# A transformer layer in fp32r matmuls: moving operands stored with even columns ahead of odd ones, and read alternately

## The chip, the cores and the metric

The kernel runs on one core of a Trainium2 chip. The metric is the device time of one execution in microseconds; smaller is better. Before the change it is 909.54 us, the median of 3 runs (909.48 to 910.15).

## The reference

One layer of a hybrid block, 512 tokens, width 1024, fp32 throughout. What is computed, cut to its core:

```python
h = rms_norm(x, mix_norm_pre)
xa, ga, q, k, v, f_logit, g_a, g_b = split(h @ w_in)
hr = rg_lru(causal_dwconv(xa, conv_a_w, conv_a_b), ...)       # recurrence over tokens, width 1280
y_a = gelu(ga) * hr
y_b = forgetting_attention(q, k, v, f_logit + b_forget)       # 16 heads of 64, causal
merged = sigmoid(g_a + b_merge[0]) * (y_a @ w_proj_a) + sigmoid(g_b + b_merge[1]) * (y_b @ w_proj_b)
x = x + rms_norm(merged @ w_out, mix_norm_post)
h = rms_norm(x, ffn_norm_pre)
gate, val = split(causal_dwconv(h @ w_up, conv_f_w, conv_f_b))  # 2 x 3072
x = x + rms_norm((gelu(gate) * val) @ w_down, ffn_norm_post)
```

## The kernel before

**Matmuls.** Each fp32 operand `a` is split into a high part (`ah`, rounded to fp32r by a cast on ACT) and a low part (`al = a - ah`, a subtraction on DVE), and a product is made of three matmuls, high by high, high by low and low by high (`mm3`, L218 to L220; the Strassen products L429 to L432; `out_matmuls` L1175 to L1177; `down_step` L1459 to L1461). A matmul has a stationary operand of 128 by 128, which a weight load (PEld) brings into the array, and a moving operand of 512 or 256 columns that streams past it from SBUF. It writes to a bank of PSUM.

**Stages.** The program goes through them in this order; PE's work follows one after another.

- xa: the input projection of the recurrent branch, weights stationary, tokens moving (512 columns, `project`); with it the gates of the recurrence (`gate_mm`).
- v: tokens stationary, weights moving. ga and pa: weights stationary, tokens moving.
- The merge gates ma and mb by Strassen's scheme (`Halved`, `Pair.product`): blocks of 256 tokens moving.
- Attention over pairs of heads: q, k, scores (`scores`, L1006), softmax on DVE and ACT, transposes of the probabilities (`pt`, L1042), A times V (`av`, L1066 and L1067), then pb.
- wo: merged tokens stationary (`mh`, `ml`), columns of `w_out` moving.
- up: the first six column tiles in halves of 256 tokens (`project_half`, L230 to L233), the others by Strassen's scheme, 84 matmuls of 256 columns a pair of tiles.
- down: seven products of Strassen's scheme, each in six steps of 12 matmuls; tokens stationary (`ah`, `al`), columns of `w_down` moving, 512 wide (the last in halves of 256).

**What sets the order.** The code's order, with a scheduler that places instructions as buffers come free, and three hand-ordered stretches (`manual_schedule`): the head, the merge gates and the Strassen part of up into down. SP issues nearly all loads; POOL issues the sums for the Strassen weights of down between DRAM buffers (`background`) and 42 adding transfers (L365). `fetch` loads and splits weights one or two units ahead of their use. `offset` tiles shift pools to chosen places in SBUF.

**Who makes the operands.** `hh`, `hl`: casts and subtractions from transposed blocks (`turned_hi`, `turned_lo`); `xh`, `xl` L519 and L520; `yh`, `yl` L773 and L774; `yb` L1073 and L1074; q and k in `halves` L992 and L993; `mh`, `ml` L1160 and L1161; the down projection's `ah` L1427 and `al` (`sub`, L325); weights in `Split` L172 and L175.

Of the kernel before, what the change touches and what calls it, by code (L numbers as in the profile page):

```python
# [57 lines left out]
NU = 3  # L58
HALO = rg_halo()
# [4 lines left out]
def kernel(  # L64
# [27 lines left out]
    cpool.tile([P, 120], F32, name="offset0")  # L92
# [17 lines left out]
    pool.memset(epst, EPS)  # L110
    cpt = cpool.tile([P, NC], F32, name="cpt")
# [110 lines left out]
    def project(dst, unit, ah, al, lo=0, hi=S):  # L222
        wh, wl = unit
        for k in range(KD):
            mm3(dst[:, lo:hi], wh[:, k], wl[:, k], ah[:, k, lo:hi], al[:, k, lo:hi], k == 0, k == KD - 1)

    def project_half(dst, unit, ah, al, c):
        wh, wl = unit
        for k in range(KD):
            pe.matmul(dst[:, c], wh[:, k], ah[:, k, c], start=k == 0, stop=False)  # L230
            pe.matmul(dst[:, c], wh[:, k], al[:, k, c], start=False, stop=False)
        for k in range(KD):
            pe.matmul(dst[:, c], wl[:, k], ah[:, k, c], start=False, stop=k == KD - 1)  # L233

    def rstd_of(ss, name):
        sd = small.tile([P, 1], F32, tag="sd", name=f"sd_{name}")
        act.activation(out=sd, in_=ss, func=AF.Sqrt, bias=epst, scale=1.0 / D)
# [65 lines left out]
    def v_mm(u, pv, w):  # L303
        wh, wl = w
        for t in range(NT):
            tok = slice(t * P, (t + 1) * P)
            for i in range(2):
                k = 2 * u + i
                pe.matmul(pv[t], hh[:, k, tok], wh[:, i], start=k == 0, stop=False)
                pe.matmul(pv[t], hh[:, k, tok], wl[:, i], start=False, stop=False)  # L310
                pe.matmul(pv[t], hl[:, k, tok], wh[:, i], start=False, stop=k == KD - 1)
# [29 lines left out]
    class Pair:  # L341
# [77 lines left out]
        def product(self, n, dst, first=False):  # L419
# [8 lines left out]
            for k in range(KH):  # L428
                pe.matmul(dst, wh[:, k], ah[:, k], start=first and k == 0, stop=False, skip_group_check=True)  # L429
                pe.matmul(dst, wh[:, k], al[:, k], start=False, stop=False, skip_group_check=True)  # L430
            for k in range(KH):
                pe.matmul(dst, wl[:, k], ah[:, k], start=False, stop=k == KH - 1, skip_group_check=True)  # L432
# [66 lines left out]
    with ExitStack() as rg:  # L499
        rt, ixt, tt = {}, {}, {}  # L500
        last_act = [None]
        with ExitStack() as r0:
# [47 lines left out]
            def gate_mm(t):  # L550
# [3 lines left out]
                for g, pg in enumerate(pgs):  # L554
                    mm3(pg, gh[:, g], gl[:, g], xh[t], xl[t], True, False)
                    if tl is None:
                        pe.matmul(pg, gh[: 3 * n, 2 + g], th[: 3 * n], start=False, stop=True)
                    else:
                        mm3(pg, gh[:n, 2 + g], gl[:n, 2 + g], th[:n], tl[:n], False, True)
# [11 lines left out]
            with tc.tile_pool(name="pre", bufs=2, side="right", reuse_waits="tile") as pre, ExitStack() as wp:  # L571
# [66 lines left out]
                def by_kind(i, c, kinds):  # L638
                    wh, wl = us[i].parts()
                    for n, (w, h, k0, k1) in enumerate(kinds):  # L640
                        for k in range(k0, k1):
                            pe.matmul(pss[i][:, c], (wh, wl)[w][:, k], (hh, hl)[h][:, k, c],
# [124 lines left out]
        def gate_out(t):  # L767
# [5 lines left out]
            act.copy(yh[t], gl)  # L773
            dve.tensor_tensor(out=yl[t], in0=gl, in1=yh[t].bitcast(F32), op=ALU.subtract)  # L774
# [29 lines left out]
        def forget():  # L804
# [10 lines left out]
            for k in range(KD):  # L815
                pe.matmul(pf[0:48], fw[:, k], hh[:, k], start=k == 0, stop=False)
                pe.matmul(pf[0:48], fw[:, k], hl[:, k], start=False, stop=k == KD - 1)
# [11 lines left out]
            dve.tensor_scalar(out=cum, in0=cum, scalar1=-8.0, scalar2=None, op0=ALU.mult)  # L829
            for b in range(NT):  # L830
                nc.sync.dma_start(cnd[:, PO[b] : PO[b + 1]], cum[:, : PO[b + 1] - PO[b]])
# [42 lines left out]
        for step, (e, half) in enumerate(PA_ORDER):  # L874
# [3 lines left out]
            for i in range(5):  # L878
                k = 5 * half + i
                mm3(pps[e], wh[:, i], wl[:, i], yh[k], yl[k], k == 0, k == TR - 1)  # L880
# [32 lines left out]
    def prep_alloc(p):  # L913
# [71 lines left out]
    with ExitStack() as at:  # L985
# [3 lines left out]
        def halves(ps, name):  # L989
            hi = apool.tile([P, S], F32R, tag=f"{name[0]}h", name=f"h_{name}", bufs=1)  # L990
            lo = apool.tile([P, S], F32R, tag=f"{name[0]}l", name=f"l_{name}", bufs=1)
            rounded.append(act.copy(hi, ps))  # L992
            dve.tensor_tensor(out=lo, in0=ps, in1=hi.bitcast(F32), op=ALU.subtract)  # L993
# [63 lines left out]
        def av(p, pts):  # L1057
# [15 lines left out]
            act.copy(yb[p][:, 0], y)  # L1073
            dve.tensor_tensor(out=yb[p][:, 1], in0=y, in1=yb[p][:, 0].bitcast(F32), op=ALU.subtract)  # L1074
# [3 lines left out]
        def pb_part(e, ks):  # L1078
# [7 lines left out]
            for k in ks:  # L1086
                mm3(pb[e], wh[:, k], wl[:, k], yb[k][:, 0], yb[k][:, 1], k == 0, k == KD - 1)
# [40 lines left out]
        for e in range(2):  # L1128
            for w in pbw[e]:
                pe.matmul(pb[e], w[:, i], yb[i][:, 0], start=False, stop=False)  # L1130
        for e in range(2):
            pe.matmul(pb[e], pbw[e][0][:, i], yb[i][:, 1], start=False, stop=False)
# [21 lines left out]
    for e in range(KD):  # L1154
# [14 lines left out]
    def out_matmuls(acc, toks, k, ah, al, wh, wl, nk, halves=(0, 1)):  # L1169
        for t in toks:  # L1170
            tok = slice(t * P, (t + 1) * P)
            for hf in halves:
                c = slice(512 * hf, 512 * hf + 512)
                dst = acc[t][hf]
                pe.matmul(dst, ah[:, tok], wh[:, c], start=k == 0, stop=False)  # L1175
                pe.matmul(dst, ah[:, tok], wl[:, c], start=False, stop=False)
                pe.matmul(dst, al[:, tok], wh[:, c], start=False, stop=k == nk - 1)  # L1177
# [7 lines left out]
    with ExitStack() as mix:  # L1185
# [12 lines left out]
        def mix_norm(t, acc):  # L1198
# [9 lines left out]
            rs = rstd_of(ss, f"mix{t}")  # L1208
# [213 lines left out]

    def y_hi(i):
# [3 lines left out]
        act.copy(yhl[i][0], yhl[i][2])  # L1427

    def y_lo(i):
        sub(yhl[i][1], yhl[i][2], yhl[i][0].bitcast(F32))  # L1430
# [321 lines left out]
```

## Time and profile before

| what | value |
|---|---|
| median of 3 runs | 909.54 us (909.48 to 910.15) |
| the profiled execution: its span, first to last instruction | 908.0 us |
| DMA, mean over the span | 204 GB/s |
| DVE, subtraction of a down weight, 128x1024 (L175), each | 1218 ns |
| ACT, cast of a down weight, 128x1024 (L172), each | 1051 ns |

The profiled execution is one further execution; its span is the time from its first to its last instruction, and runs are timed around more than the span. PE is the matmul stream, PEld the weight loads, which overlap it; DVE, ACT and POOL are the vector, scalar and GpSimd engines, SP issues DMAs. A matmul's duration in the trace (389 ns at 512 columns) holds its passage through the pipeline; the pace is the distance from one start to the next. L numbers are lines of the kernel before.

### The profile page before, as it was taken

Reading aid. Unit: us, or ns where it says so; the run is one execution under the profiler, and the core shown is the slowest. Engines: PE = TensorE matmul, PEld = TensorE weight load, DVE = VectorE, ACT = ScalarE, POOL = GpSimd, SP = SyncE. Lnnn points to the kernel's source line nnn. Section 1 sums busy time; section 2 is a strip of 40 time slices with the busy share of each in tenths; the row PEclk is TensorE's granted clock in tenths of the full one; section 3 lists DMA queues with packets and bytes.
Section 4 is the critical chain, followed back from the end, with each engine's and each line's share of the span. In section 5 each row is a group of like instructions: output and inputs, shape, how many; then the busy total and the mean of one; then the engine's idle time right before and its main releaser. Section 6 shows DMA issues by size and latency. Waiting matters only on the chain.

```text
span 908.0 us, 15830 instructions
## 1 busy us (share of the span) xinstructions
PE 899.4 (99%) x5856; PEld 800.0 (88%) x5856; DVE 739.0 (81%) x1209; ACT 594.9 (66%) x1031; POOL 215.9 (24%) x277
## 2 busy tenths in 40 slices
PE   9999999999999999999999999999999999999997
PEld 7888888878899998888888889999999999988886
DVE  7976469638878749888778588999999999889897
ACT  6565595433466648776654487878888888677564
POOL 4244335544110112212104100233323223100000
PEclk9999999999999999999999999999999999999999
DMA  6877589989964377434415654578888988699764
GB/s 262 260 232 201 163 210 277 249 224 185 203 164 160 95 241 278 154 132 159 160 63 174 205 183 145 141 185 210 237 208 220 238 203 212 210 395 328 245 203 146
DMA packets 71040, 185.24 MB, mean 204 GB/s; under 512 B 7153, under 2 KB 27681, under 8 KB 70578
## 3 DMA queue, kind: packets, MB, share of 16 engines
q1 hardware_dynamic: 47360, 127.72, 41.7%
q0 software_dynamic: 23456, 56.37, 28.7%
q8 instruction: 46, 0.75, 0.3%
q14 instruction: 32, 0.26, 0.1%
q10 hardware_dynamic: 146, 0.14, 0.0%
HBM read 150.69 MB, written 35.73 MB: 205 GB/s over the span
## 4 chain that ended last, share of the span: by engine, by line
PE 99%; DVE 0%; ACT 0%; issue 0%; DVEq 0%
PE up L430 7%; PE up L432 7%; PE up L429 7%; PE dn L1461 4%; PE dn L1460 4%; PE dn L1459 4%; PE pa L218 2%; PE ga L220 2%; PE ga L218 2%; PE pa L219 2%; PE pa L220 2%; PE ga L219 2%; PE k L218 2%; PE q L218 2%; PE wo L1175 2%; PE pb L218 2%
## 5 line engine op out<-in xcount | busy, mean ns | idle before, releaser
L1336 DVE SCALAR_TENSOR_TENSOR u<-up,cpt,u 128x511 f32<-128x511 f32 x96 | 71.3, 745 | 3.5 <-ACT u L1330 1.8
L365 POOL DMA_DIRECT2D ml<-raw_up x42 | 36.2, 862 | 153.8 <-ACT ml L364 90.4
L1461 PE MATMUL dn<-wh_dn,al 128*128 128x512 f32 (+1 forms) x180 | 67.6, 376 | 0.0
L1459 PE MATMUL dn<-wh_dn,ah 128*128 128x512 f32 (+1 forms) x180 | 67.5, 375 | 0.0
L1460 PE MATMUL dn<-wl_dn,ah 128*128 128x512 f32 (+1 forms) x180 | 67.5, 375 | 0.0
L429 PE MATMUL up<-sh,th 128*128 128x256 f32 x252 | 60.2, 276 | 0.0
L430 PE MATMUL up<-sl,th 128*128 128x256 f32 x252 | 60.2, 276 | 0.0
L175 DVE TENSOR_TENSOR wl_dn<-raw_dn,wh_dn 128x1024 fp32r<-128x1024 f32 x42 | 51.1, 1218 | 9.7 <-ACT wh_dn L172 9.6
L172 ACT CAST wh_dn<-raw_dn 128x1024 fp32r<-128x1024 f32 x42 | 44.1, 1051 | 20.0 <-issue 8.0
L1330 ACT ACTIVATE u<-up,cpt 128x512 f32<-128x512 f32 x48 | 37.0, 780 | 22.2 <-PE up L432 12.0
L325 DVE TENSOR_TENSOR tl<-t,th 128x1024 fp32r<-128x1024 f32 x42 | 51.1, 1217 | 0.0
L430 PEld LDWEIGHTS up<-sl,th 128*128 128x128 f32 x252 | 47.3, 188 | 0.0
L429 PEld LDWEIGHTS up<-sh,th 128*128 128x128 f32 x252 | 47.3, 188 | 0.0
L411 ACT CAST th<-t 128x1024 fp32r<-128x1024 f32 x42 | 43.8, 1045 | 2.2
L1344 POOL TENSOR_TENSOR yf<-u,u 128x512 f32<-128x512 f32 x23 | 30.6, 1332 | 61.1 <-issue 48.1
L429 PE MATMUL up<-h2h,mh 128*128 128x256 f32 x168 | 40.2, 276 | 0.0
L430 PE MATMUL up<-h2l,mh 128*128 128x256 f32 x168 | 40.2, 276 | 0.0
L1461 PEld LDWEIGHTS dn<-wh_dn,al 128*128 128x128 f32 x180 | 33.9, 188 | 6.3 <-DVE al L325 0.3
L1459 PEld LDWEIGHTS dn<-wh_dn,ah 128*128 128x128 f32 x180 | 33.9, 188 | 6.1
L1460 PEld LDWEIGHTS dn<-wl_dn,ah 128*128 128x128 f32 x180 | 33.9, 188 | 6.1
L432 PE MATMUL up<-sh,tl 128*128 128x256 f32 x252 | 38.8, 276 | 0.0
L1020 ACT ACTIVATE P<-P,mx 128x384 f32<-128x384 f32 (+3 forms) x64 | 35.2, 552 | 5.4 <-DVE mx L1015 4.5
(728 smaller groups left out, 3220.6 us busy)
## 6 DMA issues: line engine op xcount, KB each, us to landing
raw_up<-in_w_up_dram SPq DMA_DIRECT2D x48, 512.0 KB, 5.3
td<-in_w_down_dram POOLq DMA_DIRECT2D x36, 512.0 KB, 6.0
raw_dn<-td SPq DMA_DIRECT2D x24, 512.0 KB, 5.1
ml<-raw_up POOLq DMA_DIRECT2D x21, 512.0 KB, 5.4
B<-cnd POOLq DMA_DIRECT2D x16, 640.0 KB, 5.5
raw_dn<-in_w_down_dram SPq DMA_DIRECT2D x18, 512.0 KB, 3.7
raw_wo<-in_w_out_dram SPq DMA_DIRECT2D x16, 512.0 KB, 4.2
td<-td POOLq DMA_DIRECT2D x12, 512.0 KB, 11.7
```

What stands on the lines that cost most here:

```text
L172: act.copy(self.wh, self.raw)
L175: engine.tensor_tensor(out=self.wl, in0=self.raw, in1=self.wh.bitcast(F32), op=ALU.subtract)
L218: pe.matmul(dst, ah, bh, start=first, stop=False)
L325: dve.tensor_tensor(out=out, in0=a, in1=b, op=ALU.subtract)
L411: act.copy(self.th[i], self.t[i])
L429: pe.matmul(dst, wh[:, k], ah[:, k], start=first and k == 0, stop=False, skip_group_check=True)
L430: pe.matmul(dst, wh[:, k], al[:, k], start=False, stop=False, skip_group_check=True)
L432: pe.matmul(dst, wl[:, k], ah[:, k], start=False, stop=k == KH - 1, skip_group_check=True)
L1336: dve.scalar_tensor_tensor(out=c[:, s:], in0=ps[:, : S - s], scalar=col(C_CFW + 3 * e + j), in1=c[:, s:], op0=ALU.mult, op1=ALU.add)
L1459: pe.matmul(d[:, x], ah[:, k, tok], wh[:, k, x], start=first, stop=False, skip_group_check=True)
L1460: pe.matmul(d[:, x], ah[:, k, tok], wl[:, k, x], start=False, stop=False, skip_group_check=True)
L1461: pe.matmul(d[:, x], al[:, k, tok], wh[:, k, x], start=False, stop=last, skip_group_check=True)
```

## The change

The tensors that stream past the array in the projections are stored so that of each group of columns the even ones come first and the odd ones behind them; the matmuls then read them alternately, first even, first odd, second even, second odd, so that the results in PSUM stand in the natural order. Groups are 128 columns wide for tokens that were transposed from `x` (halves of 64 columns, 256 bytes apart) and 512 wide elsewhere (halves of 256 columns, 1,024 bytes apart).

Three helpers make views: `turns` is the reading order of the matmuls; `parted` reads a naturally ordered tile evens first; `placed` names the places in the stored order, in which a write runs on.

- Tokens: the rows of `x` are brought into the order by the host's layout, in blocks of 128, so hidden states and `v` have it on their own; the result's rows are put back at the end.
- Weights that move (`w_in`'s v part, `w_out`, `w_down`): columns ordered in the host's layout (`spread`). Weights that are stationary are as before.
- `xh/xl`, `yh/yl`, `yb`, k, `mh/ml` and the down projection's `ah/al`: written in the order by the casts on ACT and the subtractions on DVE that make them, whose input is then read with a step of two elements. Of these, `xh/xl`, `yh/yl` and `yb` are moving operands; k, `mh/ml` and `ah/al` are read in line, and are ordered so that their tokens match the rows of `v` and `x`.
- Attention: keys are in the order, so the bias over keys (`cnd`, from a new tile `keys`) and the mask (`affine_select`) are too. The scores, the transposes and A times V read as before, q is as before.
- `mh` and `ml` lose the factor 0.5 (a plain cast and a plain subtraction in place of a scaled copy and a scalar_tensor_tensor); the norm behind `wo` takes four times its epsilon for it (`eps4`, a new constant; `offset0` shrinks by 32 bytes).

On every engine the instructions stand in the same order as before; beside the access patterns only these rows differ: eight of ACT and eight of DVE for `mh` and `ml`, the tile names of `keys` and `eps4`, and one memset more on POOL.

```diff
+HT = 64
+def turns(ap, d=HT):
+    if ap.shape[-1] == 2 * d:
+        return ap.rearrange("p (a i) -> p i a", a=2)
+    return ap.rearrange("p (t a i) -> p t i a", a=2, i=d)
+def parted(ap, d=HT):
+    if ap.shape[-1] == 2 * d:
+        return ap.rearrange("p (i a) -> p a i", a=2)
+    return ap.rearrange("p (t i a) -> p t a i", a=2, i=d)
+def placed(ap, d=HT):
+    if ap.shape[-1] == 2 * d:
+        return ap.rearrange("p (a i) -> p a i", a=2)
+    return ap.rearrange("p (t a i) -> p t a i", a=2, i=d)
...
-    cpool.tile([P, 120], F32, name="offset0")
+    cpool.tile([P, 112], F32, name="offset0")
...
+    eps4 = cpool.tile([P, 1], F32, name="eps4")
+    pool.memset(eps4, 4 * EPS)
...
     def project(dst, unit, ah, al, lo=0, hi=S):
-            mm3(dst[:, lo:hi], wh[:, k], wl[:, k], ah[:, k, lo:hi], al[:, k, lo:hi], k == 0, k == KD - 1)
+            mm3(dst[:, lo:hi], wh[:, k], wl[:, k], turns(ah[:, k, lo:hi]), turns(al[:, k, lo:hi]), k == 0, k == KD - 1)
...
-                pe.matmul(pv[t], hh[:, k, tok], wh[:, i], start=k == 0, stop=False)
+                pe.matmul(pv[t], hh[:, k, tok], turns(wh[:, i], SH), start=k == 0, stop=False)
...
-                pe.matmul(dst, wh[:, k], ah[:, k], start=first and k == 0, stop=False, skip_group_check=True)
+                pe.matmul(dst, wh[:, k], turns(ah[:, k]), start=first and k == 0, stop=False, skip_group_check=True)
...
             def split_a(t):
-                act.copy(xh[t], xc[t])
-                dve.tensor_tensor(out=xl[t], in0=xc[t], in1=xh[t].bitcast(F32), op=ALU.subtract)
+                act.copy(placed(xh[t], SH), parted(xc[t], SH))
+                dve.tensor_tensor(out=placed(xl[t], SH), in0=parted(xc[t], SH), in1=placed(xh[t].bitcast(F32), SH),
+                                  op=ALU.subtract)
...
-            dve.tensor_scalar(out=cum, in0=cum, scalar1=-8.0, scalar2=None, op0=ALU.mult)
+            keys = tl("keys")
+            dve.tensor_scalar(out=placed(keys), in0=parted(cum), scalar1=-8.0, scalar2=None, op0=ALU.mult)
...
+                diag = placed(diag)
                 pool.affine_select(out=diag, in_=diag, compare_op=ALU.is_ge, fill=NEG, base=0,
-                                   pattern=[[-1, P]], channel_multiplier=1)
+                                   pattern=[[-1, 2], [-2, HT]], channel_multiplier=1)
...
+            if name[0] == "k":
+                rounded.append(act.copy(placed(hi), parted(ps)))
+                dve.tensor_tensor(out=placed(lo), in0=parted(ps), in1=placed(hi.bitcast(F32)), op=ALU.subtract)
...
-        act.activation(out=mh[:, e], in_=tg, func=AF.Copy, scale=0.5)
-        dve.scalar_tensor_tensor(out=ml[:, e], in0=tg, scalar=0.5, in1=mh[:, e].bitcast(F32),
-                                 op0=ALU.mult, op1=ALU.subtract)
+        act.copy(placed(mh[:, e]), parted(tg))
+        dve.tensor_tensor(out=placed(ml[:, e]), in0=parted(tg), in1=placed(mh[:, e].bitcast(F32)), op=ALU.subtract)
...
     def y_hi(i):
-        act.copy(yhl[i][0], yhl[i][2])
+        act.copy(tokens(yhl[i][0], placed), tokens(yhl[i][2], parted))
     def y_lo(i):
-        sub(yhl[i][1], yhl[i][2], yhl[i][0].bitcast(F32))
+        sub(tokens(yhl[i][1], placed), tokens(yhl[i][2], parted), tokens(yhl[i][0].bitcast(F32), placed))
...
-                    pe.matmul(d[:, x], ah[:, k, tok], wh[:, k, x], start=first, stop=False, skip_group_check=True)
+                    bh, bl = turns(wh[:, k], SH)[:, h], turns(wl[:, k], SH)[:, h]
+                    pe.matmul(d[:, x], ah[:, k, tok], bh, start=first, stop=False, skip_group_check=True)
...
+    def spread(w):
+        return w.reshape(w.shape[0], -1, HB, 2).transpose(0, 1, 3, 2).reshape(w.shape)
+    HB = 256
+    r = {"x": f("x").reshape(NT, HT, 2, D).transpose(0, 2, 1, 3).reshape(S, D), "w_out": spread(f("w_out"))}
```

`turns` stands in the same way on the moving operands of `project_half`, `gate_mm`, the first xa tiles, the forget logits, pa, pb and `out_matmuls`.

More of the change, by code (lines that the diff above doesn't have):

```diff
@@ L229, in project_half, with rstd_of @@
         for k in range(KD):
-            pe.matmul(dst[:, c], wh[:, k], ah[:, k, c], start=k == 0, stop=False)
-            pe.matmul(dst[:, c], wh[:, k], al[:, k, c], start=False, stop=False)
+            pe.matmul(dst[:, c], wh[:, k], turns(ah[:, k, c]), start=k == 0, stop=False)
+            pe.matmul(dst[:, c], wh[:, k], turns(al[:, k, c]), start=False, stop=False)
         for k in range(KD):
-            pe.matmul(dst[:, c], wl[:, k], ah[:, k, c], start=False, stop=k == KD - 1)
-    def rstd_of(ss, name):
+            pe.matmul(dst[:, c], wl[:, k], turns(ah[:, k, c]), start=False, stop=k == KD - 1)
+    def rstd_of(ss, name, eps=epst):
         sd = small.tile([P, 1], F32, tag="sd", name=f"sd_{name}")
-        act.activation(out=sd, in_=ss, func=AF.Sqrt, bias=epst, scale=1.0 / D)
+        act.activation(out=sd, in_=ss, func=AF.Sqrt, bias=eps, scale=1.0 / D)
         rs = small.tile([P, 1], F32, tag="rs", name=f"rs_{name}")
@@ L308, in v_mm @@
                 k = 2 * u + i
-                pe.matmul(pv[t], hh[:, k, tok], wh[:, i], start=k == 0, stop=False)
-                pe.matmul(pv[t], hh[:, k, tok], wl[:, i], start=False, stop=False)
-                pe.matmul(pv[t], hl[:, k, tok], wh[:, i], start=False, stop=k == KD - 1)
+                pe.matmul(pv[t], hh[:, k, tok], turns(wh[:, i], SH), start=k == 0, stop=False)
+                pe.matmul(pv[t], hh[:, k, tok], turns(wl[:, i], SH), start=False, stop=False)
+                pe.matmul(pv[t], hl[:, k, tok], turns(wh[:, i], SH), start=False, stop=k == KD - 1)
     def v_out(c, pv):
@@ L815, in forget @@
             for k in range(KD):
-                pe.matmul(pf[0:48], fw[:, k], hh[:, k], start=k == 0, stop=False)
-                pe.matmul(pf[0:48], fw[:, k], hl[:, k], start=False, stop=k == KD - 1)
+                pe.matmul(pf[0:48], fw[:, k], turns(hh[:, k]), start=k == 0, stop=False)
+                pe.matmul(pf[0:48], fw[:, k], turns(hl[:, k]), start=False, stop=k == KD - 1)
             z = tl("z")
@@ L1129 @@
             for w in pbw[e]:
-                pe.matmul(pb[e], w[:, i], yb[i][:, 0], start=False, stop=False)
+                pe.matmul(pb[e], w[:, i], turns(yb[i][:, 0], SH), start=False, stop=False)
         for e in range(2):
-            pe.matmul(pb[e], pbw[e][0][:, i], yb[i][:, 1], start=False, stop=False)
+            pe.matmul(pb[e], pbw[e][0][:, i], turns(yb[i][:, 1], SH), start=False, stop=False)
         pb_part(2, range(KD - 1))
@@ L1174, in out_matmuls @@
                 dst = acc[t][hf]
-                pe.matmul(dst, ah[:, tok], wh[:, c], start=k == 0, stop=False)
-                pe.matmul(dst, ah[:, tok], wl[:, c], start=False, stop=False)
-                pe.matmul(dst, al[:, tok], wh[:, c], start=False, stop=k == nk - 1)
+                pe.matmul(dst, ah[:, tok], turns(wh[:, c], SH), start=k == 0, stop=False)
+                pe.matmul(dst, ah[:, tok], turns(wl[:, c], SH), start=False, stop=False)
+                pe.matmul(dst, al[:, tok], turns(wh[:, c], SH), start=False, stop=k == nk - 1)
     ups = Halved("", lambda e: w_up[int(e[2:])], h2h, h2l)
@@ L1421, in load_first, with tokens @@
         nc.sync.dma_start(yraw[1, m], yd[m][:, :, X])
+    def tokens(y, order):
+        return order(y.rearrange("p k c -> p (k c)"))
     def y_hi(i):
@@ L1724, in _lay_out @@
     r["w_up"] = blocks(f("w_up"), D, P)
-    down = f("w_down").reshape(2, DF // 2, D)
+    down = spread(f("w_down")).reshape(2, DF // 2, D)
     r["w_down"] = np.concatenate([blocks(d[:, c : c + D // 2], 2 * P, D // 2) for d in down for c in (0, D // 2)])
@@ L1750 @@
     r = _run(nc, [arrays], core_ids=[0])
-    return r.results[0]["out_0_dram"][None]
+    rows = r.results[0]["out_0_dram"].reshape(NT, 2, HT, D)
+    return rows.transpose(0, 2, 1, 3).reshape(1, S, D)
```

43 lines of the change are left out of this document (23 added, 20 removed).

## The prediction

> **What bounds the kernel now.** I read the page's first part, then the chain that ended last, then who waited, and last a table of stretches. The first fence has lines of the page, the second the list of cores, the third the waits of PE (us in all, times, longest).
>
> ```profile
> span 908.0 us, 15830 instructions
> PE 899.4 (99%) x5856; PEld 800.0 (88%) x5856; DVE 739.0 (81%) x1209; ACT 594.9 (66%) x1031; POOL 215.9 (24%) x277
> PE 99%; DVE 0%; ACT 0%; issue 0%; DVEq 0%
> ```
> ```profile
> core 0: 908.0 us, clock 0.998
> ```
> ```profile
> PE xa L596 <- DVE ones L599: 1.5, 1, 1.5
> PE xa L642 <- ACT hh L250: 0.4, 1, 0.4
> PE k L218 <- DVE mx L1015: 0.2, 1, 0.2
> ```
>
> The chain is matmuls, and the three waits of PE come to 2.1 us in 908. Nothing that makes another engine faster can help; the time is the number of matmuls times their pace. The clock is granted in full. The other engines' room is read by stage (busy us and instructions of PE, of the weight loads PEld, of DVE, ACT, POOL; then clock, DMA share, GB/s):
>
> ```profile
> 18.00:133.00 115.00, 115.00 (x531) 95.85 (x530) 79.48 (x124) 73.66 (x119) 45.02 (x47) 1.00 0.70 204
> 133.00:188.00 55.00, 55.00 (x244) 45.57 (x243) 41.89 (x64) 27.59 (x52) 24.38 (x28) 1.00 1.04 268
> 188.00:246.00 58.00, 58.00 (x257) 46.88 (x257) 39.73 (x48) 19.53 (x29) 22.62 (x26) 1.00 0.94 199
> 246.00:257.00 11.00, 11.00 (x52) 9.17 (x51) 11.00 (x12) 8.91 (x11) 0.90 (x1) 1.00 0.38 118
> 257.00:333.00 76.00, 76.00 (x659) 76.00 (x659) 54.53 (x77) 45.83 (x75) 9.20 (x17) 1.00 0.54 157
> 333.00:476.00 143.00, 142.83 (x1050) 120.15 (x1049) 119.46 (x329) 96.99 (x247) 23.83 (x70) 1.00 0.48 166
> 564.00:788.00 224.00, 224.00 (x1958) 223.52 (x1957) 206.77 (x304) 181.78 (x277) 65.08 (x65) 1.00 0.80 205
> 788.00:891.00 103.00, 103.00 (x472) 85.72 (x471) 92.64 (x117) 71.81 (x102) 2.94 (x4) 1.00 0.84 283
> ```
>
> The two long last stages matter: in the up projection (564 to 788) DVE is busy 92% and the weight loads all the time; in the down projection (788 to 891) DVE is busy 90%.
>
> **The pace of a matmul.** The next rows are the timeline of PE (start us, duration us). The first two are the first matmul of the ga stage and of the pa stage after it, with 240 matmuls of 512 columns between them; the three others lie in the spin at the start.
>
> ```profile
> 133.20 0.39 PE L218 MATMUL ga<-hh,wh_ga 128*128 128x512 f32 x1
> ...
> 187.60 0.39 PE L218 MATMUL pa<-yh,wh_pa 128*128 128x512 f32 x1
> ```
> ```profile
> 2.48 0.63 PE L596 MATMUL xa<-ones 128*128 128x512 f32 x1
> 2.90 0.63 PE L596 MATMUL xa<-ones 128*128 128x512 f32 x1
> 3.33 0.63 PE L596 MATMUL xa<-ones 128*128 128x512 f32 x1
> ```
>
> 54.40 us by 240 is 226.7 ns. In the spin a matmul of the same form starts every 0.425 us (0.85 by 2), nearly twice that; I read this as an array at half its clock, though the granted clock, 0.998 over the span, does not set this stretch apart. At full clock the same columns would then take about 213 ns. The measured 226.7 is 17/16 of 213.3: a surplus of 6%, one clock in 16 columns, which is 64 bytes of a 4-byte operand. At half the clock there is no such surplus: 0.425 would be 0.453. So the surplus is not the array's own; something that feeds it falls just short at full clock. At 256 columns the up stage gives the same share: 224.00 us by 1,957 is 114.5 ns, against about 107.
>
> **What the change does, and its price.** No instruction is added to PE's stream, none moves on any queue, and all tiles keep their places. What changes is in which order addresses are read.
>
> (1) 5,104 of the 5,856 matmuls read their moving operand alternately from two streams, 256 or 1,024 bytes apart. By the loops of the code these are 2,212 of 512 columns (xa 192, v 192, ga 240, pa 240, f 16, gates of the recurrence 96, q and k 384, pb 192, wo 192, down 468) and 2,892 of 256 (the first two xa tiles 96, merge gates 672, up 2,052, down 72). The transposes, scores, A-times-V and spin keep their reads. No row of this trace has an alternating moving read, so the price is bounded from both sides: at best the surplus goes whole (213 ns), at worst each column pays its own step (below, the first rival). I take the good end. A shortfall that comes once in 64 consecutive bytes, at full clock only, looks like one stream waiting for its own next piece, and two streams read in turn leave each piece twice the time. This is an inference; the chances below carry its doubt.
>
> At 512 columns: 2,212 times 13.3 ns is 29.5 us.
>
> At 256 columns another row sets a floor, the weight loads. The fence has PE and then PEld in one A-times-V group; the last row sums up a run of transposes.
>
> ```profile
> 398.22 0.23 PE L1066 MATMUL av<-PTh,v 128*128 128x128 f32 x1
> 398.28 0.27 PE L1067 MATMUL av<-PTl,v 128*128 128x128 f32 x1
> 398.39 0.44 PE L1066 MATMUL av<-PTh,v 128*128 128x512 f32 x1
> ```
> ```profile
> 398.22 0.19 PEld L1067 LDWEIGHTS av<-PTl,v 128*128 128x128 f32 x1
> 398.33 0.19 PEld L1066 LDWEIGHTS av<-PTh,v 128*128 128x128 f32 x1
> 398.44 0.19 PEld L1067 LDWEIGHTS av<-PTl,v 128*128 128x128 f32 x1
> ```
> ```profile
> 8.28:9.92 1.64, 1.64 (x17) 1.64 (x15) 1.32 (x3) 1.00 (x3) 1.64 (x2) 1.00 1.01 415
> ```
>
> A matmul of 128 columns is followed after 0.06 us, and the next only after 0.11, with the loads 0.11 apart; the transposes pass 15 loads in 1.64 us, 109 ns each. A load of 128 columns hardly comes oftener than every 110 ns. So 256 columns come from 113.3 (the 226.7 halved) to about 110: 2,892 times 3.3 ns is 9.6 us. Without that floor it would be 2,892 times 6.7, 19.3 us, my good bound; no gain at all the other.
>
> (2) 86 casts on ACT and 86 subtractions on DVE (xh/xl 10, yh/yl 10, yb 8, k 8, mh/ml 8, the down projection's ah/al 42) read every second element, and write in two runs. No row of before reads so. The nearest are the same instructions read in order (mean ns of one before the last bar):
>
> ```profile
> L175 DVE TENSOR_TENSOR wl_dn<-raw_dn,wh_dn 128x1024 fp32r<-128x1024 f32 x42 | 51.1, 1218 | 9.7 <-ACT wh_dn L172 9.6
> L325 DVE TENSOR_TENSOR al<-q,ah 128x512 fp32r<-128x512 f32 x36 | 24.6, 682 | 0.0
> ```
> ```profile
> L172 ACT CAST wh_dn<-raw_dn 128x1024 fp32r<-128x1024 f32 x42 | 44.1, 1051 | 20.0 <-issue 8.0 <-PE dn L1461 4.9 <-DMA raw_dn<-td 2.9
> L1427 ACT CAST ah<-q 128x512 fp32r<-128x512 f32 x36 | 22.1, 615 | 0.4 <-DVE q L325 0.3
> ```
>
> A column costs DVE 1.05 ns (1218 less 682, by 512) and ACT 0.85. Reading the same elements at a wider step can't be quicker than reading them in line, so the bounds are nothing and a second slot for each column, 0.54 us an instruction on DVE and 0.44 on ACT. I take a third, 0.18 on DVE, nearer to the rows there are. It matters only in the down stage: some 40 of them add 7.2 us to DVE's 92.64, 99.8 against the 96.6 that PE would need there (103 less 6.4). That gives back 3 us. At the full slot it is 92.64 and 21.6, 114 us, and the down stage alone becomes 11 us longer than now. ACT with a full slot would have 71.81 and 17.6, under 97, hidden. In the attention DVE has 23 us of room and the 16 instructions at most 9.
>
> [...]
>
> (3) Small: the 64 selects on POOL get a two-run pattern (POOL is busy 24 of 143 us in that stage, so twice their time is hidden), ml's eight instructions become plain subtractions, one memset and one tile are added. Nothing each. In 246 to 257 DVE is busy 11.00 of 11.00, so its 48 matmuls gain nothing: 0.6 back. About 1 us more I leave for the last 17 us, where DVE and ACT end the kernel.
>
> In the up stage the 6.8 us of gain (2,052 times 3.3) leave 217 us for DVE's 206.8: it still fits, with 10 us of room where it now has 17.
>
> **The sum.** 29.5 and 9.6, less 3.0, 0.6 and 1.0, is 34.5 us. From the profiled 908.0 that is 873.5; the runs' median, 909.54, lies 1.5 above this span, so the forecast is 875.0 us.
>
> **Rivals.**
>
> *The step costs* (slower). The surplus could be the opposite: the price of going from one piece to the next, paid once in 16 columns in a row. Then alternate reading goes to another piece at every column. If p clocks are the price of a step, a matmul takes (1 + p) times its 213 or 107 ns; it decides from p = 1/16, where the time equals the present one. At p = 1, 512 columns take 427 ns: 2,212 times 200 ns and 2,892 times 100 are 732 us more, 1,641 in all; at a quarter of a clock 2,212 times 40 and 2,892 times 20 give 1,056. For it: no row shows that alternate reads are free. Against it: the surplus is absent at half the clock, where a fixed price in clocks would stay, and a waiting time need not. Chance 0.20.
>
> [...]
>
> *The pace stays* (the change doesn't do what it says). If the shortfall is one of bytes over time, or of the PSUM side, the order of addresses is indifferent: 226.7 and 113.3 stay. Then 909.5 as long as DVE's stepping reads take at most the third assumed (99.8 of 103 us in the down stage), and 920 at the full slot, 11 us more. For it: the share is the same at 256 and 512 columns. Chance 0.12, of which 0.08 lies within 0.2% and 0.04 above.
>
> *DVE takes the gain back* (a smaller gain). With the full slot in (2), the gain outside the down stage (39.1 less 6.4 and 1.6, 31) less 11 there leaves 20: 889.5. *No floor under the loads*: 9.7 us more, 865. Both belong to the case of the forecast.
>
> **Chances and range.** Forecast's case 0.68, from 860.7 (29.5 and 19.3 whole, nothing given back) to 890; pace stays 0.12; step costs 0.20. For 8 in 10 the range takes in the first two, 860 to 920, and leaves the third out. The likeliest case's own range is 860 to 890. Within 0.2%, or 1.8 us, is what a measurement of this kernel can't tell from no change: faster 0.68, same 0.08, slower 0.24.
>
> **What would show it.** Right: the ga stage's 240 matmuls in 51.2 us in place of 54.4; the up stage in about 217, its weight loads 110 ns apart, with PE still without waits; al's subtraction at about 0.86 us and the first waits of PE on wl_dn or al in the down stage. Floor wrong: up at 211. Stepping reads wrong: al at 0.68 or over 1.2 us. Wrong altogether: ga at 54.4 us (pace stays) or above (step costs).

## The result, and the profile after

The changed kernel takes 886.32 us, the median of 4 runs (886.20 to 887.06), where the kernel before takes 909.85 us in runs beside it (909.48 to 910.17). The ratio is 0.974, with a 95% interval of 0.973 to 0.976. It is faster by 23.5 us; the forecast was 34.5 us.

The first fence has the page's lines on the span, the engines and the chain that ended last.

```profile
span 884.6 us, 15833 instructions
...
PE 871.0 (98%) x5856; PEld 794.5 (90%) x5856; DVE 744.6 (84%) x1209; ACT 611.1 (69%) x1031; POOL 215.4 (24%) x278
...
PE 85%; DVE 9%; ACT 2%; issue 2%; DMA 1%; DVEq 0%; SPq 0%; ACTq 0%
```

The span fell by 23.4 us. The chain was 99% PE; now 9% of it goes through DVE, so PE is no longer the bound everywhere. The waits of PE (us in all, times, longest) say where:

```profile
PE dn L1500 <- DVE al L351: 1.2, 6, 0.4
PE q L246 <- DVE wl_q L201: 0.9, 1, 0.9
PE up L256 <- ACT hf L293: 0.7, 1, 0.7
PE dn L1499 <- DVE wl_dn L201: 0.4, 1, 0.4
```

These are idle times, counted from the modelled end of a matmul, which lies some 0.16 us behind the point at which the next could have started (0.38 us long at 512 columns, where the next starts after 0.22). What PE really loses is larger; below I count it from start to start, as the time by which a matmul's successor comes later than the pace of its width (where that is over 8 ns). In the down stage that is 4.4 us after, 0.2 before.

**Pace at 512 columns.** The timeline of PE (start us, duration us), first matmuls of ga and of pa:

```profile
127.53 0.38 PE L244 MATMUL ga<-hh,wh_ga 128*128 128x512 f32 x1
...
179.33 0.38 PE L244 MATMUL pa<-yh,wh_pa 128*128 128x512 f32 x1
```

51.80 us by 240 is 215.8 ns. Before it was 54.40 us; the forecast was 51.2, or 213.3 ns.

**Pace at 256 columns.** The up stage runs from its first matmul to the first of the down stage. The next two fences have these four, before and after, from the timelines of PE.

```profile
551.02 0.28 PE L230 MATMUL up<-h2h,wh_up 128*128 128x256 f32 x1
...
784.93 0.39 PE L1459 MATMUL dn<-wh_dn,ah 128*128 128x512 f32 x1
```
```profile
532.04 0.27 PE L256 MATMUL up<-h2h,wh_up 128*128 128x256 f32 x1
...
762.24 0.38 PE L1498 MATMUL dn<-wh_dn,ah 128*128 128x512 f32 x1
```

233.91 us became 230.20: 3.7 us over 2,052 matmuls, 1.8 ns each, where the forecast had 3.3 ns and 6.8 us. A wait of 0.7 us for ACT's `hf` at the start is part of it; with waits left out the pace went from 113.9 to 111.7 ns. On the prediction's own stretch, 224.00 us of this stage, the same matmuls now take 219.7 us, where it had 217, and 211 without a floor. The blocks of 256 tokens of the merge gates gained more. The next fences have, before and after, two matmuls of ma with 240 from the one to the other and no wait between:

```profile
262.15 0.28 PE L429 MATMUL ma<-gsh,gmh 128*128 128x256 f32 x1
...
289.89 0.28 PE L429 MATMUL ma<-hh,gth 128*128 128x256 f32 x1
```
```profile
251.99 0.28 PE L455 MATMUL ma<-gsh,gmh 128*128 128x256 f32 x1
...
278.79 0.28 PE L455 MATMUL ma<-hh,gth 128*128 128x256 f32 x1
```

That is 115.6 ns before and 111.7 after. The prediction had taken 113.3 ns for every matmul of 256 columns before; read in line they came at 113.9 ns in up, 115.8 in the merge gates, 117.7 in xa and 119.7 in down. The weight loads of the changed kernel in the middle of the up stage (start us, duration us):

```profile
650.13 0.19 PEld L456 LDWEIGHTS up<-h2l,mh 128*128 128x128 f32 x1
650.24 0.19 PEld L455 LDWEIGHTS up<-h2h,mh 128*128 128x128 f32 x1
650.35 0.19 PEld L456 LDWEIGHTS up<-h2l,mh 128*128 128x128 f32 x1
```

They come 0.11 us apart, without a gap between matmuls: the floor is there. In nanoseconds the mean distance of two matmuls is 111.7, not 110.

**The stepping casts.** In the groups of instructions (busy us, mean ns of one, idle before), al and ah of the down stage:

```profile
L351 DVE TENSOR_TENSOR al<-q,ah 128x512 fp32r<-128x512 f32 x36 | 29.5, 820 | 0.0
```
```profile
L1464 ACT CAST ah<-q 128x512 fp32r<-128x512 f32 x36 | 31.4, 871 | 5.5 <-DVE q L1574 4.6 <-DVE q L351 0.5 <-DMA q<-yd 0.3
```

al went from 682 to 820 ns, ah from 615 to 871. In the table of stretches (PE, loads, DVE, ACT, POOL, clock, DMA share, GB/s) the end of up and most of down read:

```profile
552.00:769.50 217.50, 217.14 (x1922) 216.15 (x1921) 203.20 (x297) 179.74 (x272) 65.71 (x65) 1.00 0.84 211
769.50:869.00 99.50, 98.31 (x460) 84.20 (x459) 94.10 (x116) 79.47 (x99) 2.01 (x3) 1.00 0.86 288
```

DVE is busy 94.10 of 99.5 us in the down stage, and 4.2 us of what PE newly loses lie there, more than in any other stage.

### The profile page after: what moved, and what is told of

Its sections match the earlier page's. It is cut to its first block, busy times and chain, and to the rows that moved or that the text cites. A ratio compares the mean times of both kernels' runs of the same rounds, so it can differ in the third digit from the quotient of the medians.

```text
span 884.6 us, 15833 instructions
## 1 busy us (share of the span) xinstructions
PE 871.0 (98%) x5856; PEld 794.5 (90%) x5856; DVE 744.6 (84%) x1209; ACT 611.1 (69%) x1031; POOL 215.4 (24%) x278
## 4 chain that ended last, share of the span: by engine, by line
PE 85%; DVE 9%; ACT 2%; issue 2%; DMA 1%; DVEq 0%; SPq 0%; ACTq 0%
PE up L458 7%; PE up L456 7%; PE up L455 7%; PE dn L1500 2%; PE dn L1499 2%; PE dn L1498 2%; PE ga L245 2%; PE ga L244 2%; PE ga L246 2%; DVE al L351 2%; PE pa L245 2%; PE pa L244 2%; PE v L335 2%; PE v L336 2%; PE xa L244 2%
## 5 line engine op out<-in xcount | busy, mean ns | idle before, releaser
L1498 PE MATMUL dn<-wh_dn,ah 128*128 128x512 f32 (+1 forms) x180 | 65.7, 365 | 0.0
L1378 POOL TENSOR_TENSOR yf<-u,u 128x512 f32<-128x512 f32 x23 | 30.4, 1323 | 58.8 <-issue 46.0
```

The source lines that it names most:

```text
L1498: pe.matmul(d[:, x], ah[:, k, tok], bh, start=first, stop=False, skip_group_check=True)
```

## Experiments

**1. Does the reading make the pace, and what do the stepping casts cost without it?** All layouts and casts stay as changed; only the matmuls read their operands in line again, so the columns of the results come in the order of storage.

```diff
 def turns(ap, d=HT):
-    if ap.shape[-1] == 2 * d:
-        return ap.rearrange("p (a i) -> p i a", a=2)
-    return ap.rearrange("p (t a i) -> p t i a", a=2, i=d)
+    return ap
...
-                    bh, bl = turns(wh[:, k], SH)[:, h], turns(wl[:, k], SH)[:, h]
+                    bh, bl = wh[:, k, x], wl[:, k, x]
```

> The changed kernel, with the same storage order, host layouts and stepping casts, but each moving operand read in line (columns come out in another order, so this leaves out the right order of columns). Theory (the alternate read itself makes the pace): 512 columns go back to 226.7 ns and 256 to 113.3 or a little more, 909 to 914 us, and what it lies above 909.5 is the price of the stepping casts. Rival (the new storage, places or data make the pace): it stays at 215.8 and 111.6, about 886 us.

Measured: 909.73 us against 909.9, ratio 1.000 (0.999 to 1.001). The pace is back at 226.7 ns, and at 113.9 for the 256 columns of the up stage, and the chain is 99% PE. The group of al in this kernel:

```profile
L349 DVE TENSOR_TENSOR al<-q,ah 128x512 fp32r<-128x512 f32 x36 | 24.6, 683 | 0.0
```

This is the same stepping subtraction as in the changed kernel, and it takes 683 ns, not 820; ah takes 660 ns, not 871. So the whole gain comes from the read order of the matmuls. The step by itself costs DVE nothing (682 before) and ACT 45 ns (615 before): the casts are dear only while PE reads alternately.

**2. What do the dear casts of the down stage cost the kernel?** y's casts run in line; the tokens of the last product then stand in natural order.

```diff
-        act.copy(tokens(yhl[i][0], placed), tokens(yhl[i][2], parted))
+        act.copy(yhl[i][0], yhl[i][2])
...
-        sub(tokens(yhl[i][1], placed), tokens(yhl[i][2], parted), tokens(yhl[i][0].bitcast(F32), placed))
+        sub(yhl[i][1], yhl[i][2], yhl[i][0].bitcast(F32))
```

> The changed kernel, but the down projection's ah and al are cast and subtracted in line (their tokens then stand in the natural order, which leaves out the reordering of tokens). Theory (the stepping casts take back 4 us in the down stage, where PE now waits 4.4 us): al back from 820 to 682 ns, ah from 871 to 615, PE's waits in the stage under 1 us, 882 us. Rival (DVE is too full there at the new pace whatever the casts cost): the waits stay, 885 to 886 us.

Measured: 884.61 us, ratio 0.972 (0.970 to 0.974), span 883.5. al is at 682 and ah at 616 ns, and PE's loss in the down stage falls from 4.4 to 2.3 us. The kernel gains 1.1 us of span: less than the stage, because a wait in the merge gates (ma, 2.0 us in this trace, 0.5 in that of the changed kernel) took some back. Half of the down stage's loss stays: with a faster PE, DVE is late there even with cheap casts, busy 89.93 of 98.5 us. So the truth lies between the expectation and its rival, and the 882 us expected were missed by 2.6.

**3. The same, with the order made one step earlier.** The multiplication that forms y writes the tokens in the stored order, so y's casts are made in line, as in experiment 2, and the tokens keep the changed kernel's order.

```diff
-        (dve if j == JF - 1 else pool).tensor_tensor(out=y, in0=g, in1=v, op=ALU.mult)
+        (dve if j == JF - 1 else pool).tensor_tensor(out=placed(y), in0=parted(g), in1=parted(v), op=ALU.mult)
...
```

> The down projection's tokens are put in order one step earlier, in the product of gate and value (23 on POOL, 1 on DVE: reads with a step of two, writes two runs), and ah and al are made in line. Theory (POOL has room): as with in-line casts, 882 us; POOL's product may go from 1.32 us to at most 2.6 us, 30 us more in a stage with some 150 us of POOL idle. Rival (the taps on ACT wait for POOL to give up a buffer, 7 us in all already, and the up stage turns late): 886 us or more.

Measured: 884.68 us, ratio 0.972 (0.971 to 0.974), span 883.1. On POOL the product grows from 1323 to 1564 ns, which the other engines' work hides. The 882 us expected were missed by 2.7, and the interval just overlaps that of the changed kernel (0.973 to 0.976).

**4. Which read orders are fast?** Into the kernel before I put 16 matmuls for each of 25 read orders, near its start, on a tile of ones.

```diff
+for _ in range(16): pe.matmul(pw, ones[:, :P], fl[:, 0:512], start=True, stop=True)
+v = lambda x, d: x.rearrange("p (a i) -> p i a", i=d)
+for _ in range(16): pe.matmul(pw, ones[:, :P], v(fl[:, 0:512], 256), start=True, stop=True)
...
+for _ in range(16): pe.matmul(pw, ones[:, :P], fl[:, 0:1024].rearrange("p (i a) -> p i a", a=2)[:, :, 0], start=True, stop=True)
...
```

> The kernel before, with 40 matmuls to warm up and then 16 matmuls of each of 26 read orders at its start, on a tile of ones that nothing else reads; their paces are read from the trace. Theory A (a stream waits for its own next 64 bytes; two streams give each twice the time): in line 226.7 ns; alternate 215.8 at 64 bytes and more apart; a step of 2 crosses 64 bytes twice as often, 240 ns, of 4 266 ns, of 8 320 ns; evens then odds 240; alternate in runs of 2, 4 and 16 215.8. Theory B (neighbouring columns from one word or line are what costs, any order without them is quick): step 2, 4, 8 and evens then odds 215.8 too, runs of 2 and 4 and 16 back towards 226.7. Rival C (a clash with the weight loads): with a stationary operand of 64 columns, half the load, 512 alternate stays but 256 in line and alternate fall from 113.3 and 111.6 to about 109; if they stay, the loads are no floor at 256.

PE's timeline groups the 16 (start us, us in all). In order of lines: in line, alternate with the streams 1024, 256, 64, 16, 8 and 128 B apart, and every second column.

```profile
17.48 3.79 PE L607 MATMUL xa<-hh,ones 128*128 128x512 f32 x16
21.11 3.62 PE L608 MATMUL xa<-hh,ones 128*128 128x512 f32 x16
24.56 3.62 PE L609 MATMUL xa<-hh,ones 128*128 128x512 f32 x16
28.01 3.62 PE L610 MATMUL xa<-hh,ones 128*128 128x512 f32 x16
31.47 3.62 PE L611 MATMUL xa<-hh,ones 128*128 128x512 f32 x16
34.92 3.83 PE L612 MATMUL xa<-hh,ones 128*128 128x512 f32 x16
38.59 3.62 PE L613 MATMUL xa<-hh,ones 128*128 128x512 f32 x16
42.04 7.46 PE L614 MATMUL xa<-hh,ones 128*128 128x512 f32 x16
```

From one start to the next, by 16: 226.9 ns in line, 215.6 at 1024 B and at 16 B, 229.4 at 8 B. So 16 B apart is as good as 1024, and 8 B is as bad as in line. My reason in the prediction, a stream that waits for its next 64 bytes, can't be: two streams 16 B apart lie within the same 64 bytes and the surplus is gone. The other orders (means of 15 distances, ns): every second column 454.5, every fourth 461.1, every eighth 431.3, evens and then odds 451.1, alternate in runs of two 334.3, of four 250.7, of sixteen 240.4, four streams 282.3, eight 489.2. Both theories of the expectation missed here: for every second column the one had 240 and the other 215.8.

The same block sizes a matmul's fixed part. Alternate reads of 512 and 384 columns take 215.8 and 162.3 ns; 256 columns take 111.7, and 109.1 with a stationary operand of 64 columns instead of 128 (in line 119.5 and 115.1, where the expectation had 113.3 and 109). So 128 columns more cost 53.2 to 53.5 ns (256 with the narrower operand to 384, 384 to 512); by that 512 columns are 213 to 214 ns, and some 2.5 ns of each of these matmuls don't go with its width, an estimate from the three. That a narrower stationary operand helps at 256 columns (109.1 against 111.7) shows that the load of 128 is the bound there.

**5. More read orders. And who slows the casts?** The second block of extra work has more read orders, bf16 among them, and then eight casts of 512 columns on one engine at a time beside one kind of matmul (`step` reads every second column, `half` writes two runs, `v` is the alternate order).

```diff
+pe.matmul(pss[2], ones[:, :P], o, start=True, stop=True)
+dve.tensor_copy(out=got, in_=pss[2][:, 0:1])
+for _ in range(8): dve.tensor_tensor(out=half(o), in0=step(a), in1=half(b), op=ALU.subtract)
+for _ in range(48): pe.matmul(pw, ones[:, :P], v(fl[:, 0:512], 256), start=True, stop=True)
...
```

> The kernel before with blocks of extra 512-column matmuls near its start. First part, ns from start to start (read in line 226.7, alternate 215.8). [...] Second part, eight casts of 512 columns on DVE (subtraction) or ACT (copy), from a tile in order or in steps of two, beside PE idle, reading in line, or alternate at 1024, 256 or 16 B. Theory, contention: DVE 683 in all, but 820 to 840 in steps beside alternate reads; ACT 620 in order, 655 in steps, 870 beside alternate reads. Rival, the cost came from elsewhere (DMA, POOL, the other engine's casts): no form differs by more than 30 between the reads. Open: whether 16 B costs casts as much as 256 B.

Read orders, in ns: each column twice 215.8; alternate by 24 B 212.9 for 504 columns, alternate by 12 B 268.7 for 510; four streams within 64 B 268.4; bf16 in line 216.3, step 2 225.9, step 4 450.6, alternate by 8 B 216.8 and by 4 B 215.8. Bf16 in two streams of 256 columns, 512 B apart, takes 484, though fp32r in two streams of 256 columns takes 215.8.

The casts, first DVE in order beside matmuls in line (L633) and alternate at 1024 B (L637), then in steps beside matmuls in line (L652), alternate at 1024 B (L656), 256 B (L660) and 16 B (L664):

```profile
L656 DVE TENSOR_TENSOR hl<-hl 128x512 fp32r<-128x512 f32 x8 | 6.6, 829 | 0.2
L660 DVE TENSOR_TENSOR hl<-hl 128x512 fp32r<-128x512 f32 x8 | 6.6, 829 | 0.2
...
L637 DVE TENSOR_TENSOR hl<-hl 128x512 fp32r<-128x512 f32 x8 | 5.5, 691 | 0.2
L652 DVE TENSOR_TENSOR hl<-hl 128x512 fp32r<-128x512 f32 x8 | 5.5, 691 | 0.2
...
L633 DVE TENSOR_TENSOR hl<-hl 128x512 fp32r<-128x512 f32 x8 | 5.5, 691 | 0.2
...
L664 DVE TENSOR_TENSOR hl<-hl 128x512 fp32r<-128x512 f32 x8 | 5.5, 691 | 0.2
```

ACT in steps, beside alternate reads at 1024 B (L694), in line (L690) and alternate at 16 B (L702), and in order beside alternate reads at 1024 B (L675):

```profile
L694 ACT CAST hl<-hl 128x512 fp32r<-128x512 f32 x8 | 7.0, 877 | 0.2
...
L690 ACT CAST hl<-hl 128x512 fp32r<-128x512 f32 x8 | 5.3, 658 | 0.2
L702 ACT CAST hl<-hl 128x512 fp32r<-128x512 f32 x8 | 5.2, 650 | 0.2
...
L675 ACT CAST hl<-hl 128x512 fp32r<-128x512 f32 x8 | 4.9, 618 | 0.2
```

Beside matmuls in line the array first ran at half its clock. The stretches of the step casts of DVE there (columns as above):

```profile
153.50:156.50 3.00, 3.00 (x8) 2.31 (x7) 2.86 (x6) 0.00 (x0) 0.00 (x0) 0.50 0.00 0
157.00:159.10 2.10, 2.10 (x11) 1.74 (x10) 2.00 (x4) 0.00 (x0) 0.00 (x0) 1.00 0.00 0
```

In the first the granted clock is 0.50 and a matmul comes every 427 ns, in the second it is 1.00 and 227. The casts take 680 to 694 ns in both, so the comparison holds, and experiment 1 has it at full clock throughout.

829 and 877 ns here, 820 and 871 in the changed kernel: the same slowdown, with nothing running but PE and the one engine. It came only with both a cast in steps and alternate matmul reads 256 or 1024 B apart: casts in order stay at 691 and 618 ns beside these reads, casts in steps at 691 and 658 beside reads in line. PE stays at 215.8 ns in every such block, so the engine that casts pays alone. At 16 B it pays nothing (691 and 650), which experiment 6 turns into a kernel.

**6. The streams 16 bytes apart, in the kernel.** Every group of eight columns is stored evens first; the casts still step by two.

```diff
-HT = 64
+HT = 4
...
 def turns(ap, d=HT):
-    if ap.shape[-1] == 2 * d:
-        return ap.rearrange("p (a i) -> p i a", a=2)
-    return ap.rearrange("p (t a i) -> p t i a", a=2, i=d)
+    return ap.rearrange("p (t a i) -> p t i a", a=2, i=HT)
...
-    HB = 256
+    HB = HT
```

> The changed kernel with one number altered: the two streams of the alternate read lie 16 B (four columns) apart throughout instead of 256 B or 1024 B, so that the order changes only within eight columns; the same casts still step by two. Theory, contention by distance: PE keeps 215.8 and 111.6 ns, the casts go back to al 683 to 695, ah 645 to 665, xl and yl about 690, ml about 1065, the down stage's PE stalls from 4.4 to 2.0 to 2.5 us, those of ma, mb and q from 3.0 to about 1, and the kernel ends at 881.5 to 884.5 us, 0.9968 to 0.9946 of the changed kernel. Rival, the casts' steps cost by themselves or by another engine's doing: al stays at 820, 886 to 887 us. Rival, finer steps cost in their own right (four-dimensional patterns on DVE, ACT or PE): al above 850 or PE above 218 ns, over 888 us.

The changed kernel ran beside it once more:

> The changed kernel once more, on the same chip as the 16 B variant, so that the two can be compared: 886.3 us, 0.974 of before, by every theory.

Measured: 885.50 us (884.83 to 886.34) against 886.78 (885.69 to 888.56); against before 0.973 (0.972 to 0.974) and 0.974 (0.973 to 0.976). Its groups of al and of ah:

```profile
L342 DVE TENSOR_TENSOR al<-q,ah 128x512 fp32r<-128x512 f32 x36 | 24.6, 682 | 0.0
```
```profile
L1455 ACT CAST ah<-q 128x512 fp32r<-128x512 f32 x36 | 23.9, 665 | 1.5 <-DVE q L342 1.2 <-DVE q L1564 0.2
```

The casts are cheap again, as the contention theory has it, and the down stage loses 1.9 us where the changed kernel on the same chip loses 4.3. The time lies 1.0 us above the expected 881.5 to 884.5. Of the 2.4 us gained, 1.1 go to the attention, where A times V now comes before its probabilities are ready (2.1 us lost against 1.0), and the waits of ma (2.0) and q (1.6), which I had expected to shrink to 1 together, are as in the repeated run of the changed kernel: they have nothing to do with the stepping casts. Experiments 2, 3 and 6 all come out 1 to 2 us under the changed kernel; the intervals overlap, so that is their size, not an order among them.

**7. By which distance?** A third block: the stepping casts beside alternate reads at nine distances and beside reads of every second column, and more read orders.

> The kernel before with two blocks of extra work near its start. First part, ns from start to start. [...] Second part, the stepping casts beside alternate reads at distances of 16 to 1088 B. Theory, banks: the cost hangs on where the two streams lie against each other, with a period, so that 1024 plus 16, 32 or 64 B costs as little as 16, 32 or 64 B does (DVE 691, ACT 650) while 256 B and 1024 B cost 829 and 877. Rival, distance: two streams far apart keep two regions busy, so that 1040, 1056 and 1088 B cost as 1024 B does and the cost sets in at one distance between 16 and 256 B. [...]

DVE in steps beside alternate reads 128 B (L636), 256 B (L640), 1024 B (L644) and 1040 B (L648) apart:

```profile
L644 DVE TENSOR_TENSOR hl<-hl 128x512 fp32r<-128x512 f32 x8 | 6.7, 836 | 0.2
L640 DVE TENSOR_TENSOR hl<-hl 128x512 fp32r<-128x512 f32 x8 | 6.6, 829 | 0.2
L636 DVE TENSOR_TENSOR hl<-hl 128x512 fp32r<-128x512 f32 x8 | 5.5, 691 | 0.2
...
L648 DVE TENSOR_TENSOR hl<-hl 128x512 fp32r<-128x512 f32 x8 | 5.5, 691 | 0.2
```

16, 32, 64 and 128 B cost DVE nothing; 256 and 1024 B do; 1040, 1056 and 1088 B again nothing (ACT in the same order: 650, 655, 659, 669; 877, 877; 668, 668, 669). So it isn't that dear reads begin at one distance: of the distances of 16 to 1088 B tried, the two that are whole multiples of 256 B are dear, and 1040 to 1088 B are not. Matmuls that read every second column, at 454 ns, slow no cast (691, 649).

Read orders, in ns: each column four times 216.1. Two streams with each column twice 284.2, where alternate runs of two took 334.3 in experiment 4. bf16 alternate 1024 or 16 B apart 485, in runs of two 271, of four 226.8.

**8. Each width alone.** Alternate reads for the 256-column matmuls only, then for the 512-column ones only; the 72 of 256 columns in the down stage go with the 512s in both. The first of them:

```diff
 def turns(ap, d=HT):
+    if ap.free_size() == S:
+        return ap
...
-                    bh, bl = turns(wh[:, k], SH)[:, h], turns(wl[:, k], SH)[:, h]
+                    bh, bl = wh[:, k, x], wl[:, k, x]
```

> The changed kernel with every matmul of 512 columns reading in line again and those of 256 columns still alternate; layouts and stepping casts stay. It leaves the columns of the 512-column results in the order of storage. Theory, the gains add, each by its own pace: 512 columns back to 226.7 ns, 256 columns at 111.6; with the down stage's PE stalls gone, since its reads are in line (4.4 us back to under 0.5) and its casts cheap again (al about 690), span near 908.0 less 7.1, 900 to 902, time 901.5 to 903.5. Rival, the loads of weights were the bound of 256 columns already, and the gain there came with the 512s: 256 columns back to 113.3, 908 to 910.

> The counterpart: matmuls of 256 columns read in line again, those of 512 columns alternate. It leaves the columns of the 256-column results in the order of storage. Theory: 512 columns at 215.8 ns, 2,212 of them by 10.9 ns less are 24.0 us; the down stage still gives back 4.4 us (its reads and casts are as in the changed kernel), q and av some 1.5; 256 columns back to 113.3; span 908.0 less 24.0 and plus 5 to 6, 889 to 890.5, time 890.5 to 892.5. Rival, the down stage's stalls hang on the 256-column stages too (casts ahead begin earlier or later): another 2 us either way.

Measured: 902.89 us, ratio 0.992 (0.991 to 0.994), and 893.53 us, ratio 0.982 (0.980 to 0.983). Spans of the one and of the other:

```profile
core 0: 901.3 us, clock 0.998
```
```profile
core 0: 892.7 us, clock 0.997
```

256 columns alone bring 6.7 us; al is at 682 ns there, and the down stage loses 0.5 us. 512 columns alone bring 15.3 us, with al at 831 ns and 4.0 us lost in the down stage. The second lies 1.0 us over the range given: its matmuls of 256 columns, read in line, take 2.3 us more than before, summed from start to start. Of these 1.8 are one wait of ma for DVE, which the expectation had left out; the waits of PE there:

```profile
PE ma L457 <- DVE ma L476: 1.6, 1, 1.6
```

It is the place that is described under "Around 246 us" below. 6.7 and 15.3 are 22.0, near the 23.4 of the whole.

## Why the prediction was right, and where it was wrong

The forecast was 875.0 with a likeliest range of 860 to 890; the time is 886.32. The direction, the bound and the place of the loss held; most terms were too favourable.

| term of the sum | predicted, us | measured, us | from |
|---|---|---|---|
| 2,212 matmuls of 512 columns | -29.5 | -24.7 | from start to start, waits left out |
| 2,892 of 256 columns | -9.6 | -8.4 | the same |
| down stage gives back | +3.0 | +4.2 | 4.4 less 0.2 before; six of the eight waits over 0.2 us begin after 860 us |
| DVE around 246 to 257 us | +0.6 | +1.6 | q 1.1, ma 0.5 over before |
| last 17 us | +1.0 | +0.9 | from the last matmul's start to the end of the span: 6.8 before, 7.7 after |
| not in the sum | 0 | +3.0 | waits of mb and up 0.7 each, pb 0.6, xa and scores 0.4 each, A times V 0.2 |
| sum | -34.5 | -23.4 | span: -23.4 |

**Step (1), 512 columns: right in kind, its size off.** It stood as "at best the surplus goes whole (213 ns)", and I took that end. What is paid is 215.8: by the estimate of experiment 4 the columns at 213 to 214 ns, and 2.5 ns for each matmul. That part could not be seen in the in-line reads of before alone. 4.8 us of the 11.1 that are missing from the sum are this one.

**Step (1), 256 columns: the floor held, both ends of the size off.** The loads are the bound, as said: halving the load brings 2.6 ns more (111.7 to 109.1). I set them 110 ns apart from a run of transposes; they come at 111.7. The other end, 113.3 as half of 226.7, was wrong too: the prediction's own row had 114.5 (224.00 us by 1,957), and the trace has 113.9 to 119.7 by stage. Why in-line reads of 256 columns differ by stage stays open. The two errors nearly cancel, so that 8.4 of the 9.6 us came is luck. The rival without a floor is refuted by the up stage, 219.7 us of its 224.00 where that rival had 211.

**The reason for (1) was wrong.** "One stream waiting for its own next piece" of 64 bytes fell with the 16 B row. That the good end of the bounds nearly came true was luck, as far as this reason goes. Why one order is slower than another is not shown; what the orders cost is. In ns from start to start, 512 columns:

| read order | fp32r | bf16 |
|---|---|---|
| in line | 226.7 | 216.3 |
| alternate by 4 B | not run | 215.8 |
| alternate by 8 B | 229.4 | 216.8 |
| alternate by 16 B | 215.6 | 485 |
| alternate by 512 B | not run | 484 |
| alternate by 1024 B | 215.8 | 485 |
| each column twice, four times | 215.8, 216.1 | not run |
| every second column | 454.5 | 225.9 |
| every fourth | 461.1 | 450.6 |
| every eighth | 431.3 | not run |
| evens, then odds | 451.1 | not run |
| alternate in runs of two | 334.3 | 271 |
| alternate in runs of four | 250.7 | 226.8 |
| alternate in runs of sixteen | 240.4 | not run |

Of the two types only fp32r has the surplus in line: bf16 takes 216.3 ns there. And an order is not good or bad by itself: at 16 B apart fp32r takes 215.6 ns, its best, and bf16 485.

The row of the prediction on the spin stands. That 425 is half the clock was an inference there; experiment 5 has 427 ns in line at a granted clock of 0.50 and 227 at 1.00. Twice the 213 to 214 ns estimated for the columns is 426 to 428, so half the clock shows no surplus.

**Step (2), the casts: the size nearly right, the mechanism wrong.** I priced the step at 0.18 us on DVE, "a third" of a slot; al rose by 0.14. That the size came out near is luck too, since experiment 1 has the same steps at 683 ns: the step alone costs DVE nothing, and of the reads tried only alternate ones 256 B or 1024 B apart make it dear (829 to 836 ns, experiments 5 and 7). ACT's 0.26 us I had left hidden; in the stretch from 769.5 to 869 it raised ACT to 79.47 of 99.5, still hidden, though every al waits for its ah. The attention's k casts read PSUM, and stepping cost them nothing: 688 before and 691 after on DVE, 588 both times on ACT. The 4.4 us lost in the down stage have two parts: about 2.1 to 2.5 from dear casts, which experiments 2 and 6 win back within the stage, and about 2 because DVE, at 90% there before, can't follow a faster PE.

ACT's stepping cast goes from 650 to 877 ns as PE's two streams lie 16 or 1024 B apart, with nothing else changed (experiment 5).

**Around 246 us.** "Its 48 matmuls gain nothing" was too mild: PE now comes early to q's low weights (1.1 us lost at 234.8) and to the first Strassen block of ma. There a chain of other engines sets the time: DVE's sums, ACT's casts of them, ACT's copy gx, DVE's sum of ma, and then PE. The timelines of DVE have that last sum (start us, duration us; in brackets its idle time and what ended it), first in the changed kernel, then in its repeat:

```profile
250.06 0.43 DVE L474 TENSOR_TENSOR ma<-ma,gx 128x256 f32<-128x256 f32 x1 [1.72 <-ACT gx L462]
```
```profile
250.63 0.43 DVE L474 TENSOR_TENSOR ma<-ma,gx 128x256 f32<-128x256 f32 x1 [1.72 <-ACT gx L462]
```

PE lost 0.4 us there in the one and 1.9 in the other, where it had arrived 1.0 us sooner; both spans are 884.6 us. Between these two runs, what PE gained ahead of this place it lost there.

**The rivals.** That the pace stays, and that a step costs PE, are both refuted by 215.8 ns. The second named a true thing in the wrong place: dear steps exist, but in reads that skip columns (454 ns at every second column), not in alternate reads of two dense streams 16 B apart or more (215.8).

## What to carry to other kernels

An fp32r matmul of 512 columns that reads its moving operand in line loses about 11 of 227 ns, and gets them back when it reads two dense streams alternately, 16 B apart or more (up to 1088 B were tried); bf16 has no such loss (216.3 ns in line), and two streams 16, 512 or 1024 B apart slow it to 484 to 486 ns. Put the streams 16 to 128 B apart, where casts that read in steps kept their time here (691 ns on DVE, 650 to 669 on ACT), as at 1040 to 1088 B: at 256 and 1024 B they slow by a fifth to a third beside them (829 to 836 on DVE, 877 on ACT). When the engine that bounds a kernel gets 2.6% faster, look up every stage in which another was 90% busy before: here the down stage and the stretch around 246 us gave back 5.8 of the 33.1 us that the paces brought.

## What the runs showed of the hardware that was not expected

- Stepping reads of SBUF cost DVE nothing beside an idle PE or one that reads in line (691 ns against 691), and 829 beside alternate reads at 256 or 1024 B; casts in order are slowed in no block (691 on DVE, 618 on ACT).
- Stepping casts on DVE take 829 ns beside streams 256 B apart, 836 at 1024 B and 691 at 1040 B. Other multiples of 256 B than one and four weren't tried.
- bf16 read from two streams 512 B apart takes 484 ns where fp32r takes 215.8; at 4 and 8 B apart it takes 215.8 and 216.8.
- Matmuls of 256 columns read in line come at 113.9 to 119.7 ns in different stages, and read alternately at 111.6 to 111.7 in all of them.
